# An encoder layer on one core: the recurrence's operands in the space of the projections' input, and a 512-column matmul for the memories

## The chip, the cores and the metric

The kernel runs on one core of one Trainium2 chip. The metric is the device time of one execution in microseconds (us); a lower time is better. Two sequences, one of 512 tokens and one of 256, go through the layer together as 768 tokens. A difference of about 1% (16 us) is what a measurement of this kernel can tell from no change.

## What is computed

One encoder layer: a mixer (an RWKV-7 recurrence on half of the channels, gated linear attention, "GLA", on the other half), a cross attention to a memory of 256 rows for each sequence, and a feed-forward network, each between two RMS norms. The reference, cut to what matters here:

```python
def hybrid_mixer(h, p):
    proj = h @ p['w_in']
    rw = centred_shift(proj[..., :R_COLS], p['mu_prev'], p['mu_next']).astype(jnp.float32)
    gl = proj[..., R_COLS:].astype(jnp.float32)
    mixed = jnp.concatenate([rwkv7_group(rw, p), gla_group(gl, p)], axis=-1).astype(h.dtype)
    return mixed @ p['w_out']

def rwkv7_scan(r, w, k, v, kk, a):
    def step(S, inp):
        r_t, w_t, k_t, v_t, kk_t, a_t = inp
        sa = jnp.einsum('bhij,bhj->bhi', S, -kk_t)
        S = (S * w_t[:, :, None, :] + sa[..., None] * (kk_t * a_t)[:, :, None, :]
             + v_t[..., None] * k_t[:, :, None, :])
        return S, jnp.einsum('bhij,bhj->bhi', S, r_t)
    ...

def cross_attention(h, m, p):
    q = (h @ p['wq_x']).reshape(B, S, X_HEADS, X_HD)
    kv = (m @ p['wkv_x']).reshape(B, M, 2, X_HEADS, X_HD)
    ...

def encoder_trunk(x, mem, params):
        x = x + rms_norm(hybrid_mixer(rms_norm(x, p['g_mix_pre']), p), p['g_mix_post'])
        m = rms_norm(mem, p['g_mem'])
        x = x + rms_norm(cross_attention(rms_norm(x, p['g_x_pre']), m, p), p['g_x_post'])
        h = rms_norm(x, p['g_ffn_pre'])
        x = x + rms_norm(jnp.square(jax.nn.relu(h @ p['w_ff1'])) @ p['w_ff2'], p['g_ffn_post'])
```

The model width is 1024, the feed-forward width 4096. The recurrence has 8 heads of 64 channels and runs forward and backward in time; GLA has 4 heads.

## The kernel before

Every large product is done in split precision: an operand becomes a high part (`split`, line 143: a copy on ACT to fp32r) and a low part (a subtraction, on POOL or DVE, line 148), and `mm3` (line 241) issues three matmuls, high by high, high by low, low by high, for each 128 rows of the contraction.

The work of the mixer comes in these pieces:

- **Projections.** The normed input lies channels first in the tiles `hT_hi` and `hT_lo` (8 blocks of 128 channels by 768 tokens each, in the pool `hp`). A projection block (`rkv_early`, `gla_dense`) multiplies them by 128 columns of `w_in`: 24 matmuls of 512 columns and 24 of 256. There are 24 such blocks; `blocks` calls them in the order of its list.
- **A pair of recurrence heads, p = 0 to 3.** `begin(p)` makes decays and scaled keys (`prep`, `bonus`) and the matrices `low` (line 685); `invert(p)` inverts 32-by-32 triangles by 31 pairs of DVE operations that each wait for the one before (lines 744 and 746); `joined(p)` puts the inverses together (matmuls of lines 788 and 800, DVE copies of line 803). Their results go to DRAM.
- **Products.** `products(p, g)`, called by `prods`, loads what group g of pair p needs into a "place", a set of five operands of 2560 elements a partition (chunk states, keys, inverses), and makes the chunk matrices `sca`, `scb`, `bktp`. There are six groups and so six places.
- **Stages, q = 0 to 4.** `stage(q)` runs four `step`s. A step of up to three jobs (pair q - 1 in its second third, pair q in its first and last third) goes PE, ACT (`rh`, line 1019), PE, ACT, PE, DVE (`t1`, line 1040), and the next step needs that result. There are 48 evacuations `rh` in all: 8 in stage 0, 12 in each of stages 1 to 3, 4 in stage 4.
- **GLA heads, h = 0 to 3.** `gla_head(h)` works in the tile `arena` of the pool `gp`, half of which each head overwrites two heads later: loads, exponentials on ACT, scans on DVE, matmuls `gs`, `gkt`, `gds`, `go`, `gsum`, and a gate; the result goes to DRAM (`mixd`).
- **Memories.** `memory()` loads the normed memories of both sequences, 512 columns, into `mem_hi` and `mem_lo` (pool `mq2`); `memory_block(mem, b)`, for 16 blocks b of 128 columns of `wkv_x`, multiplies them. Each block has 24 weights, and every weight is used by two matmuls of 256 columns that follow each other (line 1104, held in order by `order_after`).
- **Output projection.** `load_split` brings `mixd` (8 pairs of tiles) and `w_out` (32 quarters of 128 by 256) in; `out_projection` multiplies with 288 matmuls of 512 columns and writes the next `hT_hi` and `hT_lo`. Then follow queries, attention and the feed-forward network, which the diff does not touch.

Memory on chip sets much of the order. A pool that is opened where another one was closed waits for the last use of the tiles that lay there. Before the change the pools stand so: `gp` (the GLA heads) is closed, then `mq1` with the places 0, 4, 1, 5, 2 is opened in its space; after stage 0 has been written, `hp` (the projections' input) is closed and `mq2` with place 3, two accumulators `ya` and the memories is opened. In program text all four GLA heads stand ahead of the first products.

The text is only the start of the order. The framework's scheduler puts each engine's instructions into one fixed sequence by priorities (`tc.high_priority`, with offsets: 6000 for joins, 4000 for steps, 3000 for products, 2000 for `begin` and `invert`) and by its own estimate of time; on the chip each engine then runs its sequence strictly in order and waits where an operand is not there. All DMAs are issued by one engine, SP, also in order.

Of the kernel before, what the change touches and what calls it, by code (L numbers as in the profile page):

```python
# [16 lines left out]
P = 128  # L17
# [15 lines left out]
def kernel(ctx: ExitStack, tc: tile.TileContext, I, y_prompt, y_sample):  # L33
# [412 lines left out]
    def rkv_early(p, i):  # L446

        ot = hp.tile([P, T], F32, tag="gd", bufs=2, name="gd")
        rkv_block(p, i, lambda c, n: ot[:, c:c + n])
        dma(rkvd[p, i], ot)  # L450
        if i == 2:
            vt = tokens_first(ot)
            for h, hs in enumerate(HS):
                for par, ps_ in enumerate(HS):
                    dma(vtd[p][h][:, :, par * 64:par * 64 + 64], vt[ps_, :, hs])

    def tokens_first(ot):

        vt = hp.tile([P, T], F32, tag="gd", bufs=2, name="gd")
        for c, n in SEQS:  # L460
            pt = psd("gvt")
            for j in range(0, n, P):
                pe.transpose(out=pt[:, j:j + P], in_=ot[:, c + j:c + j + P], identity=ident)
            with tc.high_priority():
                dve.tensor_copy(out=vt[:, c:c + n], in_=pt[:, 0:n])
        return vt.rearrange("p (j e) -> p j e", e=P)

    def gla_dense(g, i):

        c0 = (1952, 2208, 2992, 2464)[g] + i * P  # L470
        w = load_block([(w_cols(c0, P), 0)], P)
        ot = hp.tile([P, T], F32, tag="gd", bufs=2, name="gd")
# [132 lines left out]
    mp = mp_cm.__enter__()  # L605
    tts, tdz = [], []
    for d in range(2):
        t = mp.tile([P, NCH, 64], F32, tag=f"tt{d}", name=f"tt{d}")
        pool.memset(t, 0.0)
        tts.append(t)  # L610
        tdz.append(mp.tile([P, NCH, 32], F32, name=f"tdz{d}"))
    px = mp.tile([P, NCH, 66], F32, tag="px", name="px")
# [339 lines left out]
    def open_places(pool_, gs):  # L952
        for g in gs:
            t = pool_.tile([P, 2560], F32, tag=f"pl{g}", name=f"pl{g}")
            places[g] = (t[:, 0:512].rearrange("p (h u x) -> p h u x", h=2, x=64),
                         t[:, 512:1280].rearrange("p (u i x) -> p u i x", u=4, x=64),
                         t[:, 1280:1792].rearrange("p (u h x) -> p u h x", u=4, x=64),
                         t[:, 1792:2304].rearrange("p (u x) -> p u x", x=P),
                         t[:, 2304:2560].rearrange("p (u x) -> p u x", x=64))

    mq1_cm = tc.tile_pool(name="mq1", bufs=1, reuse_waits="tile")
# [45 lines left out]
    def step(st, x, j, pc):  # L1007
# [54 lines left out]
        else:  # L1062
            dve.tensor_tensor(out=o, in0=y1, in1=o, op=ALU.add)
            dve.tensor_tensor(out=o, in0=y2, in1=o, op=ALU.add)

    def finish(st, seqs=SEQS, tiles=None, mixed=None):

        p, pa = st["p"], st["ya"]
        pb, bon, gt = tiles or (mq2.tile([P, T], F32, tag="fb", name="fb"),) * 3
        a, b = seqs[0][0], seqs[-1][0] + seqs[-1][1]  # L1070
# [26 lines left out]
    def memory_block(mem, b):  # L1097

        w = load_block([(wkv[:, b * P:(b + 1) * P], 0)], P)
        pd, prev = psd("pd"), None  # L1100
        for k, (wh, wl) in enumerate(w):
            for i, (x, y) in enumerate(((wh, mem[k][0]), (wh, mem[k][1]), (wl, mem[k][0]))):
                for c0 in (0, 256):
                    prev = order_after(pe.matmul(  # L1104
                        out=pd[:, c0:c0 + 256], lhsT=x, rhs=y[:, c0:c0 + 256],
                        start=(k + i + c0 == 0), stop=(k + i + c0 == KD + 257)), prev)
        if b >= KD:
# [56 lines left out]
    joined(2)  # L1164
    invert(3)
    for b in range(16):
        memory_block(mem, b)
    stage(1)
    with tc.high_priority(offset=2000):
# [16 lines left out]
    mo = [mp.tile([P, T], F32, tag="lsb", bufs=4, name="mo") for _ in range(2)]  # L1186
    tiles = (mq2.tile([P, T], F32, tag="fb", name="fb"), *mo)
# [5 lines left out]
    mq2_cm.__exit__(None, None, None)  # L1193
    hp_cm = tc.tile_pool(name="hp2", bufs=1, side="right", reuse_waits="tile")
    hp = hp_cm.__enter__()
    for k in order:
        if k != 3:
            load_split(mixd[k], *mix[k], lo_eng=pool)
    planes = []
# [3 lines left out]
    for g in (0, 4, 1, 5):  # L1203
        t = mq1.tile([P, 5, 512], F32R, tag=f"pl{g}", name=f"w_pl{g}")
        planes += [t[:, i, :] for i in range(5)]
    planes += [mq1.tile([P, 512], F32R, tag="bkg", bufs=3, name="w_bkg") for _ in range(3)]
    t = mq1.tile([P, 5, 512], F32R, tag="pl2", name="w_pl2")
    planes += [t[:, i, :] for i in range(5)]
    wt = {}
    for i, k in enumerate(order):  # L1210
# [78 lines left out]
    with tc.tile_pool(name="op1", bufs=1, reuse_waits="tile") as op1:  # L1289
        g_pre = gain_row(op1, "g_x_pre")  # L1290

        xn = [[op1.tile([P, 512], F32, name="xn")], [t[:, 512:T] for t in mo]]
        mo = [t[:, 0:512] for t in mo]

        def rows():
            return ((rk.tile([P, T], F32, tag="k", name="res0")[:, 0:512], mq1.tile([P, T], F32, tag="ya0", name="res1")[:, 0:512]), mo, xn)

        hT_hi, hT_lo = out_projection(op1, wt, mix, x_rows, rows, g_post, x1d, g_pre)
    mq1_cm.__exit__(None, None, None)
    mp_cm.__exit__(None, None, None)  # L1300
    rk_cm.__exit__(None, None, None)
# [441 lines left out]
```

## Time and profile before

| | |
|---|---|
| median of 3 runs | 1591.46 us (1590.47 to 1599.93) |
| the profiled execution | 1596.87 us, of which its span is 1595.0 us |
| mean granted TensorE clock | 0.914 |
| ACT, POOL busy | 718.9 us (45%), 514.6 us (32%) |
| DMA | 250.35 MB, mean 157 GB/s |

PE is TensorE's matmul, PEld its weight load, which overlaps; DVE, ACT and POOL are the vector, scalar and GpSimd engines. A matmul counts as busy until its result has drained, so PE's busy share is above its share of useful work: matmuls start before their predecessors end. "PEclk" is the share of the full TensorE clock that was granted. In a row of a window, x is the number of instructions; in a row of a tile or line, the three durations are least, median and largest in ns, then come the first and the last start in us from the span's start, then shapes.

### The profile page before, as it was taken

Reading aid. Unit: us, or ns where it says so; the run is one execution under the profiler, and the core shown is the slowest. Engines: PE = TensorE matmul, PEld = TensorE weight load, DVE = VectorE, ACT = ScalarE, POOL = GpSimd, SP = SyncE. Lnnn points to the kernel's source line nnn. Section 1 sums busy time; section 2 is a strip of 40 time slices with the busy share of each in tenths; the row PEclk is TensorE's granted clock in tenths of the full one; section 3 lists DMA queues with packets and bytes.
Section 4 is the critical chain, followed back from the end, with each engine's and each line's share of the span. In section 5 each row is a group of like instructions: output and inputs, shape, how many; then the busy total and the mean of one; then the engine's idle time right before and its main releaser. Section 6 shows DMA issues by size and latency. Waiting matters only on the chain. (4 is left out here: it accounts for less than half of the span.)

```text
span 1595.0 us, 28271 instructions
## 1 busy us (share of the span) xinstructions
PE 1442.8 (90%) x10614; PEld 1246.0 (78%) x10614; DVE 1049.7 (66%) x1605; ACT 718.9 (45%) x1417; POOL 514.6 (32%) x576
## 2 busy tenths in 40 slices
PE   7999689889887889899888999996999999999996
PEld 6887578777775777778767888786999999787785
DVE  5545885497577795764455434448876676878886
ACT  5754344443333332333344354434555556544442
POOL 6416643494317342211531354420000001231223
PEclk9999798989875988888979999997999999999998
DMA  6686555556468447754452333235555447564434
GB/s 168 181 302 188 167 137 131 145 146 192 111 205 229 127 149 176 205 134 135 126 166 99 119 95 105 73 111 160 172 169 176 158 145 284 171 204 132 143 100 142
DMA packets 279565, 250.35 MB, mean 157 GB/s; under 512 B 89264, under 2 KB 227059, under 8 KB 279428
## 3 DMA queue, kind: packets, MB, share of 16 engines
q1 hardware_dynamic: 279428, 248.54, 52.1%
q8 instruction: 84, 1.38, 0.4%
q14 instruction: 53, 0.43, 0.1%
HBM read 164.11 MB, written 82.58 MB: 155 GB/s over the span
## 5 line engine op out<-in xcount | busy, mean ns | idle before, releaser
L148 POOL TENSOR_TENSOR wlo<-wraw,whi 128x256 fp32r<-128x256 f32 x192 | 176.8, 934 | 331.0 <-ACT whi L147 231.1
L247 PE MATMUL pd<-hT_hi,whi 128*128 128x256 f32 (+1 forms) x512 | 182.0, 356 | 12.6 <-DVE gd L325 8.2
L247 PE MATMUL pd<-hT_hi,wlo 128*128 128x512 f32 (+1 forms) x512 | 180.1, 354 | 4.0 <-POOL wlo L148 4.0
L247 PE MATMUL pd<-hT_lo,whi 128*128 128x256 f32 (+1 forms) x512 | 178.6, 350 | 0.3 <-DVE hT_lo L206 0.3
L1511 POOL TENSOR_TENSOR wl<-w,wh 128x1024 fp32r<-128x1024 f32 x8 | 21.2, 2649 | 329.8 <-ACT wh L1510 329.8
L247 PEld LDWEIGHTS pd<-hT_hi,whi 128*128 128x128 f32 x512 | 100.4, 196 | 27.6 <-issue 5.5
L247 PEld LDWEIGHTS pd<-hT_hi,wlo 128*128 128x128 f32 x512 | 99.6, 195 | 18.6 <-POOL wlo L148 5.3
L147 ACT ACTIVATE whi<-wraw 128x256 fp32r<-128x256 f32 x192 | 77.3, 414 | 78.2 <-PE pd L1104 22.9
L247 PEld LDWEIGHTS pd<-hT_lo,whi 128*128 128x128 f32 x512 | 100.4, 196 | 13.0 <-DVE hT_lo L206 0.5
L148 DVE TENSOR_TENSOR ul<-ur,uh 128x768 fp32r<-128x768 f32 x56 | 77.4, 1388 | 30.7 <-ACT uh L147 17.7
L147 ACT ACTIVATE uh<-ur 128x768 fp32r<-128x768 f32 x56 | 47.4, 847 | 107.8 <-PE gz L1520 52.0
L1510 ACT ACTIVATE wh<-w 128x1024 fp32r<-128x1024 f32 x64 | 67.1, 1053 | 35.9 <-PE fz L1520 24.2
L1520 PE MATMUL gx<-wh,uh 128*128 128x512 f32 x192 | 75.0, 397 | 4.3 <-DVE acc L1713 4.3
L1511 DVE TENSOR_TENSOR wl<-w,wh 128x1024 fp32r<-128x1024 f32 x56 | 68.2, 1219 | 15.1 <-ACT wh L1510 14.5
L1520 PE MATMUL gx<-wl,uh 128*128 128x512 f32 x192 | 75.9, 395 | 0.0
L1520 PE MATMUL gx<-wh,ul 128*128 128x512 f32 x192 | 75.4, 395 | 0.0
L1520 PE MATMUL fz<-hh,wh 128*128 128x384 f32 x192 | 66.0, 344 | 1.9 <-ACT wh L1510 1.9
L1511 POOL TENSOR_TENSOR wl<-ws,wh 128x1024 fp32r<-128x1024 f32 x16 | 40.6, 2536 | 79.6 <-ACT wh L1510 79.6
L1520 PE MATMUL fz<-hh,wl 128*128 128x384 f32 x192 | 65.2, 344 | 0.8 <-DVE wl L1511 0.8
L1520 PE MATMUL fz<-hl,wh 128*128 128x384 f32 x192 | 65.8, 343 | 0.0
L1510 ACT ACTIVATE wh<-ws 128x1024 fp32r<-128x1024 f32 x48 | 50.5, 1052 | 26.8 <-PE fx L1520 22.3
L1104 PE MATMUL pd<-mem_hi,whi 128*128 128x256 f32 x256 | 59.3, 308 | 1.4 <-ACT mo L1116 1.4
(476 smaller groups left out, 4306.9 us busy)
## 6 DMA issues: line engine op xcount, KB each, us to landing
w<-in_w_ff_dram SPq DMA_DIRECT2D x64, 512.0 KB
ur<-ud SPq DMA_DIRECT2D x56, 384.0 KB
wraw<-in_w_in_dram SPq DMA_DIRECT2D x108, 128.0 KB
ud<-u SPq DMA_DIRECT2D x32, 384.0 KB
ud<-us SPq DMA_DIRECT2D x24, 384.0 KB
wraw<-in_wkv_x_dram SPq DMA_DIRECT2D x64, 128.0 KB
lora<-lo_t SPq DMA_DIRECT2D x20, 384.0 KB
bkg<-bkd SPq DMA_DIRECT2D x24, 256.0 KB
```

The costliest lines, as they stand in the source:

```text
L147: act.activation(out=hi, in_=src, func=AF.Copy)
L148: (lo_eng or pool).tensor_tensor(out=lo, in0=src, in1=hi, op=ALU.subtract)
L247: pe.matmul(out=out, lhsT=a, rhs=b, start=(i == 0), stop=(i == n - 1))
L1104: prev = order_after(pe.matmul(out=pd[:, c0:c0 + 256], lhsT=x, rhs=y[:, c0:c0 + 256], start=(k + i + c0 == 0), stop=(k + i + c0 == KD + 25 ...
L1510: act.activation(out=hi, in_=t[name], func=AF.Copy)
L1511: lo_eng.tensor_tensor(out=lo, in0=t[name], in1=hi, op=ALU.subtract)
L1520: pe.matmul(out=out, lhsT=a, rhs=b, start=first and i == 0, stop=last and i == n - 1, skip_group_check=True)
```

## The change

It moves tiles, and with them work:

- The places 0, 4, 1, 5 and most of place 3 are cut out of two tiles that take over the tags, and so the space, of `hT_hi` and `hT_lo`; place 2 and a piece of place 3 stay in `mq1`, now on the right side of the memory. So `hp` is not closed, and the products wait for the last projection block instead of for the last GLA head.
- In the text the last three projection blocks stand inside the list of the blocks; `gla_head(2)`, `begin(2)`, `invert(2)` and `gla_head(3)` move from among the blocks to behind `stage(0)`, with the products of place 3. Only then is `gp` closed and `mq2`, with the memories alone, opened in its space.
- `memory_block` calls `mm3` on all 512 columns: 24 matmuls a block in place of 48.
- After the sixteenth memory block `mq2` is closed, and 18 of the 32 halves of `w_out` get tiles of their own in its space (`wo1`); before, 20 lay in the places 0, 4, 1, 5. Accumulators `ya`, `xn` and a residual row move to the projection blocks' `gd` tiles, `fb` to `sxf`.

The diff, cut:

```diff
+    gdp_cm = tc.tile_pool(name="gdp", bufs=1, side="right", reuse_waits="tile")
+    gdp = gdp_cm.__enter__()
...
-    with tc.tile_pool(name="gp", bufs=1, reuse_waits="tile") as gp:
+    gp_cm = tc.tile_pool(name="gp", bufs=1, reuse_waits="tile")
+    gp = gp_cm.__enter__()
+    if True:
...
         blocks([(5, i) for i in range(3)])
-        gla_head(2)
         blocks([(3, 3), (2, 3)])
-        begin(2)
-        invert(2)
-        gla_head(3)
+        blocks([(6, i) for i in range(3)])
...
-    open_places(mq1, (0, 4, 1, 5, 2))
-    yas = [mq1.tile([P, T], F32, tag="ya0", name="ya0")]
+    plh, pll = (hp.tile([P, KD * T], F32, tag=n, name="pl_" + n) for n in ("hh", "hl"))
+    for t, gs in ((plh, (0, 4)), (pll, (1, 5))):
+        for i, g in enumerate(gs):
+            whole_place(g, t[:, 2560 * i:2560 * i + 2560])
+    place(3, plh[:, 5120:5632], pll[:, 5120:5888], mq1.tile([P, 512], F32, tag="pl3", name="pl3"), plh[:, 5632:6144],
+          pll[:, 5888:6144])
+    whole_place(2, mq1.tile([P, 2560], F32, tag="pl2", name="pl2"))
+    yas = [gdp.tile([P, T], F32, tag="gd", bufs=2, name=f"ya{i}") for i in range(2)]
...
-        pd, prev = psd("pd"), None
-        for k, (wh, wl) in enumerate(w):
-            for i, (x, y) in enumerate(((wh, mem[k][0]), (wh, mem[k][1]), (wl, mem[k][0]))):
-                for c0 in (0, 256):
-                    prev = order_after(pe.matmul(
-                        out=pd[:, c0:c0 + 256], lhsT=x, rhs=y[:, c0:c0 + 256],
-                        start=(k + i + c0 == 0), stop=(k + i + c0 == KD + 257)), prev)
+        pd = psd("pd")
+        mm3(pd, list(zip(w, mem)))
...
     prods(0, (0, 4, 1, 5))
-    blocks([(6, i) for i in range(3)])
     stage(0)
-    prods(0, (2,))
-    hp_cm.__exit__(None, None, None)
+    prods(0, (2, 3))
+    gla_head(2)
+    begin(2)
+    invert(2)
+    gla_head(3)
+    gp_cm.__exit__(None, None, None)
     mq2_cm = tc.tile_pool(name="mq2", bufs=1, reuse_waits="tile")
     mq2 = mq2_cm.__enter__()
-    open_places(mq2, (3,))
-    yas += [mq2.tile([P, T], F32, name=f"ya{i}") for i in (1, 2)]
-    prods(0, (3,))
     mem = memory()
     begin(3)
     joined(2)
     invert(3)
     for b in range(16):
         memory_block(mem, b)
+    mq2_cm.__exit__(None, None, None)
     stage(1)
...
+    wo1_cm = tc.tile_pool(name="wo1", bufs=1, reuse_waits="tile")
+    wo1 = wo1_cm.__enter__()
+    planes = [wo1.tile([P, 512], F32R, name=f"w_out{i}") for i in range(18)]
```

What the scheduler makes of it shows best on PE. The lists below are PE's sequence; names are those of the tiles (`pd<-hT...` a projection, `gsum`, `gs`, `gds`, `go` of a GLA head, `low` of `begin`, `merge` of a join, `rec` a step), then the size of the result and a count. Ahead of the change, the last GLA head's sums stand among projections:

```order
L247 MATMUL pd<-hT_hi,wlo 128x256
L247 MATMUL pd<-hT_hi,whi 128x256
L921 MATMUL gsum<-arena,ones_f 128x512
L921 MATMUL gsum<-arena,ones_f 128x256
L247 MATMUL pd<-hT_lo,whi 128x256
L247 MATMUL pd<-hT_hi,wlo 128x256
L247 MATMUL pd<-hT_hi,whi 128x256
```

After it, behind stage 0, the sums of head 2 stand between small matmuls of `begin(2)`, `begin(3)` and head 3:

```order
L880 MATMUL gkt<-ident,arena 128x128 x6
L926 MATMUL gsum<-arena,ones_f 128x512
L926 MATMUL gsum<-arena,ones_f 128x256
L688 MATMUL low<-bk 64x64 x8
L867 MATMUL gs<-arena 64x64 x24
L634 MATMUL hsum<-kds,ones_bd 128x512
L903 MATMUL gds<-arena 128x128 x8
```

Two heads have left the projections; no projection and no memory matmul stands beside them any more. The second place is PE's first memory matmul. Before, it stands among `low` and products, ahead of stage 1:

```order
L1049 MATMUL rec<-pl_4468 64x64 x4
L991 MATMUL sca<-pl_4467,bkg 64x64
L992 MATMUL scb<-pl_4467,bkg 64x64
L685 MATMUL low<-bk 64x64
L1104 MATMUL pd<-mem_hi,whi 128x256 x2
L1104 MATMUL pd<-mem_lo,whi 128x256 x2
L685 MATMUL low<-bk 64x64 x14
```

Now it stands in the midst of stage 1, behind all of `low`, head 3 and the join of pair 2:

```order
L1032 MATMUL rec<-pl_hh 64x64 x4
L1040 MATMUL rec<-rh,pl_hh 64x64 x4
L1058 MATMUL rec<-pl_4232 64x64 x4
L249 MATMUL pd<-mem_hi,whi 128x512
L249 MATMUL pd<-mem_lo,whi 128x512
L1047 MATMUL rec<-pl_hh 64x64 x8
L1009 MATMUL bktp<-ident,bkg 128x64 x8
```

All memory blocks have moved behind it, and a row holds one matmul where it held two. The third place is the end of stage 4. Before, PE has output projection (`po<-`) between the last steps:

```order
L1023 MATMUL rec<-pl_5344 64x64 x4
L1031 MATMUL rec<-rh,pl_5344 64x64 x4
L247 MATMUL po<-w_pl_9176,mix_wc 128x512
L247 MATMUL po<-w_pl_9177,mix_wc 128x512
L247 MATMUL po<-w_pl_9176,mix_r 128x512
```

After, the steps follow the last memory matmul with nothing between, and `po` begins behind them:

```order
L249 MATMUL pd<-mem_hi,wlo 128x512
L1058 MATMUL rec<-pl_4232 64x64 x4
L1120 MATMUL kvt<-ident,mo 128x128 x4
L1027 MATMUL rec<-pl_hh,pl_hl 64x64 x4
L1032 MATMUL rec<-pl_hl,pl_hh 64x64 x4
L1040 MATMUL rec<-rh,pl_hl 64x64 x4
L1047 MATMUL rec<-pl_hh,pl_4231 64x64 x4
L1058 MATMUL rec<-pl_hh 64x64 x4
```

So the output projection has left stage 4. Counted in the same sequences: of the 48 step evacuations, 8 stand ahead of the first memory matmul before the change and 14 after it; of the 1152 matmuls of the projection blocks, 478 stand behind the join of pair 0 before, and 513 after; behind the first memory matmul up to the last step stand 384 memory matmuls and 1114 others after the change.

More of the change, by code (lines that the diff above doesn't have):

```diff
@@ L446, in rkv_early @@
     def rkv_early(p, i):
-        ot = hp.tile([P, T], F32, tag="gd", bufs=2, name="gd")
+        ot = gdp.tile([P, T], F32, tag="gd", bufs=2, name="gd")
         rkv_block(p, i, lambda c, n: ot[:, c:c + n])
@@ L457, in tokens_first @@
     def tokens_first(ot):
-        vt = hp.tile([P, T], F32, tag="gd", bufs=2, name="gd")
+        vt = gdp.tile([P, T], F32, tag="gd", bufs=2, name="gd")
         for c, n in SEQS:
@@ L471, in gla_dense @@
         w = load_block([(w_cols(c0, P), 0)], P)
[L472 removed]
+        ot = gdp.tile([P, T], F32, tag="gd", bufs=2, name="gd")
         for c, n, pd in channels_product(w, P, hT_hi, hT_lo):
@@ L605 @@
     mp = mp_cm.__enter__()
-    tts, tdz = [], []
+    tdz = mp.tile([P, 2, NCH, 32], F32, tag="tdz", name="tdz")
+    tdz = [tdz[:, d] for d in range(2)]
+    tts = []
     for d in range(2):
@@ L942, with place, whole_place @@
         blocks([(5, i) for i in range(3)])
-        gla_head(2)
         blocks([(3, 3), (2, 3)])
-        begin(2)
-        invert(2)
-        gla_head(3)
+        blocks([(6, i) for i in range(3)])
     places = {}
[L952 to L961, printed above, removed]
-    mq1 = mq1_cm.__enter__()
-    open_places(mq1, (0, 4, 1, 5, 2))
-    yas = [mq1.tile([P, T], F32, tag="ya0", name="ya0")]
+    mq1_cm = tc.tile_pool(name="mq1", bufs=1, side="right", reuse_waits="tile")
+    mq1 = mq1_cm.__enter__()
+    def place(g, xv, a_, bkt, rbk, tp):
+        places[g] = (xv.rearrange("p (h u x) -> p h u x", h=2, x=64), a_.rearrange("p (u i x) -> p u i x", u=4, x=64),
+                     bkt.rearrange("p (u h x) -> p u h x", u=4, x=64), rbk.rearrange("p (u x) -> p u x", x=P),
+                     tp.rearrange("p (u x) -> p u x", x=64))
+    def whole_place(g, t):
+        place(g, *(t[:, a:b] for a, b in ((0, 512), (512, 1280), (1280, 1792), (1792, 2304), (2304, 2560))))
+    plh, pll = (hp.tile([P, KD * T], F32, tag=n, name="pl_" + n) for n in ("hh", "hl"))
[6 more added lines that the diff above has]
+    yas = [gdp.tile([P, T], F32, tag="gd", bufs=2, name=f"ya{i}") for i in range(2)]
     def bc2(ap):
@@ L1064, in step, with finish_tile @@
             dve.tensor_tensor(out=o, in0=y2, in1=o, op=ALU.add)
+    def finish_tile():
+        return mp.tile([P, D], F32, tag="sxf", name="fb")[:, 0:T]
     def finish(st, seqs=SEQS, tiles=None, mixed=None):
         p, pa = st["p"], st["ya"]
-        pb, bon, gt = tiles or (mq2.tile([P, T], F32, tag="fb", name="fb"),) * 3
+        pb, bon, gt = tiles or (finish_tile(),) * 3
         a, b = seqs[0][0], seqs[-1][0] + seqs[-1][1]
@@ L1165 @@
     invert(3)
+    yas.append(mp.tile([P, T], F32, tag="kds", name="ya2"))
     for b in range(16):
         memory_block(mem, b)
+    mq2_cm.__exit__(None, None, None)
     stage(1)
@@ L1186 @@
     mo = [mp.tile([P, T], F32, tag="lsb", bufs=4, name="mo") for _ in range(2)]
-    tiles = (mq2.tile([P, T], F32, tag="fb", name="fb"), *mo)
+    tiles = (finish_tile(), *mo)
     with tc.high_priority(offset=2000):
@@ L1202 @@
         planes += [t[:, 0, :], t[:, 1, :]]
-    for g in (0, 4, 1, 5):
-        t = mq1.tile([P, 5, 512], F32R, tag=f"pl{g}", name=f"w_pl{g}")
-        planes += [t[:, i, :] for i in range(5)]
+    planes.append(mp.tile([P, T], F32R, tag="tdz", name="w_tdz")[:, 0:512])
     planes += [mq1.tile([P, 512], F32R, tag="bkg", bufs=3, name="w_bkg") for _ in range(3)]
@@ L1208 @@
     planes += [t[:, i, :] for i in range(5)]
+    planes.append(mq1.tile([P, 512], F32R, tag="pl3", name="w_pl3"))
     wt = {}
@@ L1290 @@
         g_pre = gain_row(op1, "g_x_pre")
-        xn = [[op1.tile([P, 512], F32, name="xn")], [t[:, 512:T] for t in mo]]
+        xn = [[gdp.tile([P, T], F32, tag="gd", bufs=2, name="xn")[:, 0:512]], [t[:, 512:T] for t in mo]]
         mo = [t[:, 0:512] for t in mo]
         def rows():
-            return ((rk.tile([P, T], F32, tag="k", name="res0")[:, 0:512], mq1.tile([P, T], F32, tag="ya0", name="res1")[:, 0:512]), mo, xn)
+            return ((rk.tile([P, T], F32, tag="k", name="res0")[:, 0:512], gdp.tile([P, T], F32, tag="gd", bufs=2, name="res1")[:, 0:512]), mo, xn)
         hT_hi, hT_lo = out_projection(op1, wt, mix, x_rows, rows, g_post, x1d, g_pre)
+    wo1_cm.__exit__(None, None, None)
     mq1_cm.__exit__(None, None, None)
+    gdp_cm.__exit__(None, None, None)
     mp_cm.__exit__(None, None, None)
```

5 lines of the change are left out of this document (removed).

## The prediction

> **What bounds the kernel now.** I read the page's head first, then a table of windows cut at the stages, then rows of single tiles.
>
> ```profile
> span 1595.0 us, 28271 instructions
> ...
> PE 1442.8 (90%) x10614; PEld 1246.0 (78%) x10614; DVE 1049.7 (66%) x1605; ACT 718.9 (45%) x1417; POOL 514.6 (32%) x576
> ```
>
> PE is busy 90%, but busy counts draining. What a matmul really occupies is the distance to the next start:
>
> ```profile
> 100.06 0.40 PE L247 MATMUL pd<-hT_hi,whi 128*128 128x512 f32 x1
> 100.30 0.39 PE L247 MATMUL pd<-hT_lo,whi 128*128 128x512 f32 x1
> 100.53 0.39 PE L247 MATMUL pd<-hT_hi,wlo 128*128 128x512 f32 x1
> 100.76 0.28 PE L247 MATMUL pd<-hT_hi,whi 128*128 128x256 f32 x1
> 100.88 0.28 PE L247 MATMUL pd<-hT_lo,whi 128*128 128x256 f32 x1
> 101.00 0.28 PE L247 MATMUL pd<-hT_hi,wlo 128*128 128x256 f32 x1
> ```
>
> 512 columns take 0.23 to 0.24 us, 256 columns 0.12. The window table (us; busy and count of PE, PEld, DVE, ACT, POOL; PEclk; DMA share; GB/s) and the marks show where PE runs like that and where it doesn't:
>
> ```profile
> 288.00:443.00 155.00, 138.00 (x1031) 116.61 (x1026) 111.19 (x146) 64.83 (x117) 81.29 (x70) 0.88 0.56 152
> 443.00:503.00 60.00, 45.27 (x641) 36.74 (x639) 45.79 (x85) 23.90 (x68) 24.04 (x22) 0.66 0.75 215
> 503.00:636.00 133.00, 118.35 (x1553) 101.20 (x1554) 100.58 (x211) 43.60 (x118) 54.69 (x48) 0.83 0.60 160
> 636.00:692.00 56.00, 48.76 (x629) 42.54 (x624) 44.59 (x128) 21.91 (x59) 12.08 (x16) 0.91 0.64 183
> 692.00:745.00 53.00, 49.06 (x674) 40.94 (x673) 22.61 (x58) 16.93 (x45) 5.83 (x8) 0.77 0.56 138
> 817.00:893.00 76.00, 71.58 (x336) 56.65 (x336) 38.64 (x69) 29.03 (x77) 12.18 (x24) 0.98 0.36 116
> 893.00:1595.00 702.00, 663.02 (x3369) 587.42 (x3367) 472.03 (x585) 338.49 (x572) 152.24 (x164) 0.97 0.45 149
> ...
> L247 PE MATMUL pd<-hT_hi,wlo x384: 274/390/795, 61.9 to 442.2; 128*128 128x512 f32 x96, 128*128 128x256 f32 x96
> L1031 PE MATMUL rec<-rh,pl x384: 218/218/362, 445.7 to 820.4; 64*64 64x64 f32 x192
> L1104 PE MATMUL pd<-mem_hi,whi x256: 274/281/581, 503.0 to 789.3; 128*128 128x256 f32 x128
> ...
> 440.87 1.11 DVE L803 COPY tt<-merge 32x384 f32<-32x384 f32 x2 [1.00 <-PE merge L800]
> 444.58 1.13 DVE L803 COPY tt<-merge 32x384 f32<-32x384 f32 x2
> ...
> 288.18 1.12 DVE L803 COPY tt<-merge 32x384 f32<-32x384 f32 x2 [0.68 <-PE merge L800]
> 631.64 1.11 DVE L803 COPY tt<-merge 32x384 f32<-32x384 f32 x2 [1.89 <-PE merge L800]
> 644.09 1.13 DVE L803 COPY tt<-merge 32x384 f32<-32x384 f32 x2
> ```
>
> Projections end at 442. The joins of pairs 0, 1 and 2 end at 289, 446 and 645 (the last two `tt` copies of each). Steps run from 446 to 820, memory matmuls from 503 to 789; the output projection fills most of 817 to 893. Behind 893 the diff touches nothing (702 us stay). From 443 to 636 DVE is busy 146.4 of 193 us: there the chain of `begin`, inverse and join on DVE sets the pace, and memory matmuls lie beside it.
>
> **The change part by part.** All marks below are of the span of 1595.0 us.
>
> *512 columns.* 768 matmuls at 0.12 become 384 at 0.235: 92 against 90 us. I take 2 us off PE; bounds 0 and 4. The rule that speaks otherwise is a rival, below.
>
> *Heads 2 and 3 leave the projections.* Their price on each engine comes from all instructions on `arena`, four heads:
>
> ```profile
> 130.00:432.00 302.00, 62.93 (x472) 54.85 (x472) 75.52 (x52) 73.64 (x100) 27.93 (x36) 0.86 0.55 145
> 286.17 1.33 DVE L932 TENSOR_TENSOR arena<-arena 128x768 f32<-128x768 f32 x1
> 367.10 0.95 DVE L932 TENSOR_TENSOR arena<-arena 128x768 f32<-128x768 f32 x1
> 430.37 1.31 DVE L932 TENSOR_TENSOR arena<-arena 128x768 f32<-128x768 f32 x1
> ```
>
> One head is 15.7 us of PE, 18.9 of DVE, 18.4 of ACT; two fall out of 288 to 443. PE: 513 projection matmuls remain behind the join of pair 0 (half of each width, 0.177 us on average): 91 us, and small matmuls, about 15, so 289 + 106 = 395 at the earliest. Latest is 442, no gain. DVE: 111.2 - 37.8 = 73.4 us, which at its share of that window (111.2 of 155) takes 102: 391, and the join behind the inverse still waits for DMAs. I take 408, nearer to the lower end, as both engines have a bound near 395: **-35** at the end of the projections and at the join of pair 1.
>
> *Places in the space of `hT`.* Loads of the first place can no longer be issued under the last projections; they wait for their last matmul, then for six DMAs that SP issues one behind the other. Before, stage 0 began 3 us behind the projections; I give it 9 (bounds 3 and 20): **+6**, so 418.
>
> *Two heads behind stage 0.* From join 1 to join 2 DVE had 146 us of work over 193 (443 to 636). Counted in its sequence, the same stretch now holds the two heads (+38) but only 7 `t1` in place of 17 and fewer products (about -35): the length stays, and join 2 comes at 601, with the late start at **606** against 636 (taking 636, the end of the first copies and of DVE's work, as mark). Bounds 580, where DVE waits for nothing, and 640.
>
> *The memories start late.* They wait for head 3's result to go out, then 16 splits:
>
> ```profile
> L148 POOL TENSOR_TENSOR mem_lo<-raw,mem_hi x16: 718/727/2177, 485.4 to 512.8; 128x256 fp32r<-128x256 f32 x16
> ```
>
> 16 at 0.73 are 12 us, with DMA and gate 20: memory begins at **626**, not 503. The cover that stage 0, `low` and the joins had from memory matmuls is gone; PE is nearly empty from stage 0's end (about 462) to 626, which costs nothing there, as DVE sets that stretch, but the 90 us must then go into the rest.
>
> *What PE has behind 626.* 384 x 0.235 = 90 us, and 1114 small matmuls. Their price is the rest of a window less its memory part:
>
> ```profile
> 636.00:692.00 56.00, 28.40 (x179) 25.10 (x180) 0.91 0.64 183
> 692.00:745.00 53.00, 17.26 (x104) 14.66 (x102) 0.77 0.56 138
> ```
>
> (48.76 - 28.40) / 450 = 45 ns and (49.06 - 17.26) / 570 = 56 ns: 50 to 62 us. So 140 to 152 us, 146; at the 90% of these two windows (97.8 of 109) 162: the last memory matmul at **788**, against 790. Two steps and a bit remain. Stage 3 and stage 4 give the length of a step:
>
> ```profile
> 745.18 0.28 ACT L1019 ACTIVATE rh<-rec 128x128 f32<-128x128 f32 x1 [1.10 <-PE rec L1018]
> 777.52 0.28 ACT L1019 ACTIVATE rh<-rec 128x128 f32<-128x128 f32 x1
> 781.06 0.28 ACT L1019 ACTIVATE rh<-rec 128x128 f32<-128x128 f32 x1 [2.21 <-PE rec L1018]
> 816.30 0.28 ACT L1019 ACTIVATE rh<-rec 128x128 f32<-128x128 f32 x1
> ```
>
> 32.3 us for four steps, 8 each: 788 + 17 = **805** for the last step against 820, **-15**. (Stage 4 took 12 a step, with output projection between; that is gone.)
>
> *The output projection.* Before, it had begun inside stage 4; now all 288 matmuls (288 x 0.235 = 68 us) follow it, and `w_out` has to wait for the memory tiles' space:
>
> ```profile
> L147 ACT ACTIVATE w_pl<-raw x24: 400/418/420, 806.2 to 825.8; 128x256 fp32r<-128x256 f32 x24
> ```
>
> These splits came as late before (806 to 826, for a last memory matmul at 790), so the wait is not new. 805 + 68 + 5 of transposes + 5 to the first split pair is 883; with stalls as before (71.6 busy of 76) 887, against 893: bounds 875 and 905. So the loss here is 9 of the 15 us gained.
>
> *Sum.* Projections -35, start of stage 0 +6, join 2 at -30; the recurrence keeps that, but the memories, 123 us late, take it back but for 15; output projection +9; the rest 0, 512 columns inside the 146: 887 - 893 = -6, and -2 for residual rows now loaded early, which I only allow 0 to 3: **-8**. The profiled execution took 1596.87 with its span of 1595.0; the median of the three runs is 1591.46, 5.4 lower. I put the difference on the median: 1591.5 - 8 = **1583**.
>
> **Rivals.**
>
> *A, faster: the recurrence alone sets the end.* If PE slips memory matmuls into the waits of steps without delaying them, 626 to 788 shrinks. Inverse 3 and stage 1 end some 59 us after join 2 (665; between 636 and 692 it took 56), then stages 2 and 3 at 32 and stage 4 at 40 us: 665 + 104 + 5 = 774, less than 805 by 31, so 1583 - 30 = 1553. For it: PE's sequence has such gaps at every step. Against it: PE had 90 to 93% busy in the windows at 636 and 692 already, with half as much memory work. The Trainium skill gives it another ground: "TensorE: Matmul & The Clock Gate", section "Back-to-back issue gap", puts sustained matmuls of 512 columns at about 131 ns; memory would then be 50 us, not 90, and the sum about 1544 to 1553. The trace has 0.23 to 0.24 for the same thing, so I give that ground nothing; A lives from the first.
>
> *B, slower: the stretch without cover gets long.* The two heads now run one behind the other with nothing dense on PE. The windows show the clock that PE then gets:
>
> ```profile
> 480.00:520.00 40.00, 28.63 (x287) 23.56 (x283) 28.03 (x41) 15.18 (x40) 31.39 (x29) 0.54 0.87 236
> ...
> L1019 ACT ACTIVATE rh<-rec x8: 277/278/278, 444.9 to 489.1; 128x128 f32<-128x128 f32 x8
> ```
>
> Heads 2 and 3 ended 81 and 63 us behind the one before. Stage 0 took 44 us and so ends at 418 + 44 = 462; two heads at 81 + 63 or at 81 each, and the 20 of splits and DMA, end at 626 to 644. At 0.54 in place of 0.86 a head's 15.7 us of PE become 25, 19 more for two: 645 to 663, 19 to 37 late, 28 in the middle: 1583 + 28 = 1611. It decides from a memory start at about 650. Against it: DVE has 96 us of other work in that stretch, behind which PE's slowness hides. The same page, section "What's actually happening", says that the clock halves after an idle window of some 3.4 us and comes back after a busy one of that length; 0.54 agrees with it, and by it the whole stretch would run at half, which is B's condition.
>
> *C, the projections do not get shorter:* bound by weight splits or by `begin(1)`, they end at 430 to 443, and all later marks move: 1583 + 25 = 1608. Against it: the two bounds near 395.
>
> **How the numbers follow.** My forecast, 1583 (1566 to 1600 by the bounds of its terms), has a chance of 0.42; A 0.27 (1540 to 1570); B 0.20 (1600 to 1622); C 0.11 (1598 to 1618). Faster by over 1% is below 1575.5, slower above 1607.4; 1% is about what a measurement of this kernel can tell from no change. Faster: A 0.27 and 0.10 of the forecast, 0.37. Slower: 0.14 of B, 0.06 of C, 0.20. The same: 0.43. The range 1551 to 1614 leaves out some 0.10 of A below and 0.08 of B and C above.
>
> **What would show it.** Last projection matmul near 408; the join of pair 2's first copies near 606; first memory matmul (128x512) near 626 at 0.235 us apart, last near 788; last `rh` near 805; first queries near 887. PE below half busy from 465 to 620. A shows as a last memory matmul before 765; B as a first one after 650; C as projections past 430. What would make it wrong is a wait in neither list: SP's DMAs for the places, queued behind ones that wait.

## The result, and the profile after

The changed kernel takes 1675.24 us (median of 4, 1667.85 to 1677.75) against 1593.98 us for the kernel before on the same chip (median of 4): a ratio of 1.0498, 95% interval 1.0448 to 1.0548. It is 5% slower, some 81 us. The forecast was 1583 us, 8 less than before, with a range of 1551 to 1614; the measured time lies outside it.

The head of the page after, with the row of PE's clock and its busy tenths in 40 slices of 41.9 us:

```profile
span 1675.4 us, 27534 instructions
...
PE 1454.5 (87%) x10230; PEld 1229.3 (73%) x10230; DVE 1047.8 (63%) x1605; ACT 719.0 (43%) x1417; POOL 499.1 (30%) x576
...
PE   7997689869957566899997999997899999999996
...
PEclk9998597989655555789997999999899999999998
```

Busy times are close to those of before; the span has grown. From 461 to 670 us (the twelfth to the sixteenth slice) PE is five to seven tenths busy at about half its clock. The marks:

| mark, us of the span | before | forecast | after |
|---|---|---|---|
| last projection matmul | 442 | 408 | 430 |
| first `rh`, stage 0 | 445 | 418 | 440 |
| last `rh` of stage 0 | 489 | 462 | 506 |
| first `rh` of stage 1 | 531 | not named | 629 |
| join of pair 2, first copies | 632 | 606 | 626 |
| first memory matmul | 503 | 626 | 661 |
| last memory matmul | 790 | 788 | 873 |
| last `rh` | 816 | 805 | 883 |
| first queries | 893 | 887 | 973 |

Windows of the changed kernel cut at its marks (columns as in the prediction):

```profile
439.00:506.00 67.00, 46.83 (x544) 38.35 (x544) 46.69 (x73) 17.18 (x46) 19.11 (x12) 0.50 0.51 143
506.00:661.00 155.00, 96.23 (x976) 77.59 (x972) 119.53 (x193) 53.89 (x107) 46.38 (x46) 0.56 0.44 116
661.00:730.00 69.00, 58.02 (x762) 44.41 (x758) 37.29 (x108) 20.43 (x63) 12.57 (x16) 0.72 0.44 111
730.00:873.00 143.00, 142.93 (x1631) 108.54 (x1630) 62.97 (x183) 62.92 (x173) 41.92 (x60) 0.99 0.48 142
873.00:973.00 100.00, 84.30 (x419) 65.30 (x420) 51.74 (x97) 39.42 (x104) 30.81 (x55) 0.88 0.43 136
973.00:1676.00 703.00, 662.45 (x3369) 585.94 (x3367) 472.56 (x586) 338.31 (x572) 152.31 (x164) 0.97 0.46 149
```

Behind 973 nothing has changed (703 us, before 702). Between the projections and the queries lie 543 us, before 451 (442 to 893). The windows show two stretches that no longer lie beside each other: from 439 to 661 DVE is busy for 166 of 222 us, and PE for 143 at about half its clock, with no memory matmul among its work; from 730 to 873 PE is busy for 142.93 of 143 us at a clock of 0.99. Following the waits back, each instruction to what released it or else to the one before it on its engine, gives the chain of each stretch by engine, in us:

```
back from the first memory matmul to 434 us: DVE 113, PE 51, DMA 29, ACT 15, issue 15, other 8
back from the last step to 661 us:           PE 183, DMA 19, DVE 15, other 7
```

What lies between shows in single rows. The first `rh` of stage 1, by ACT's timeline (start, duration, in brackets the idle time before it and what ended it):

```profile
628.71 0.28 ACT L1028 ACTIVATE rh<-rec 128x128 f32<-128x128 f32 x1 [0.45 <-PE rec L1027]
```

The matmuls `go` of the heads, whose last are those of head 3, by the rows of `arena`:

```profile
L918 PE MATMUL go<-arena x96: 314/474/529, 198.6 to 630.4; 128*128 128x64 f32 x96
```

PE's timeline has the matmuls of that first step between them:

```profile
627.42 0.61 PE L918 MATMUL go<-arena 128*128 128x64 f32 x2
627.97 0.70 PE L1027 MATMUL rec<-pl 128*64 128x64 f32 x8
628.60 0.80 PE L918 MATMUL go<-arena 128*128 128x64 f32 x2
```

And the memories, by the rows of `mem_hi`:

```profile
L249 PE MATMUL pd<-mem_hi,whi x128: 388/396/799, 661.2 to 872.1; 128*128 128x512 f32 x128
...
L150 POOL TENSOR_TENSOR mem_lo<-raw,mem_hi x16: 772/880/942, 647.5 to 660.0; 128x256 fp32r<-128x256 f32 x16
```

From 506 to 628 no step of the recurrence runs, though pair 1 had been joined at 425 and its products made by 542. The first step of stage 1 runs among the last `go` of head 3; and the memories, whose space waits for head 3, follow. Their splits begin at 647, when head 3's result has gone out (644.6). Their first matmul needed only the first of these splits and its weights, which were there at 654.8; it came at 661 because a step stands ahead of it in PE's order, and that step waited for DVE:

```profile
660.56 0.69 PE L1058 MATMUL rec<-pl 128*64 128x64 f32 x8 [3.57 <-DVE t L1049]
661.19 0.80 PE L249 MATMUL pd<-mem_hi,whi 128*128 128x512 f32 x1
```

### The profile page after: what moved, and what is told of

It is laid out like the page before. It is cut to its first block, busy times and chain, and to the rows that moved or that the text cites. A ratio compares the mean times of both kernels' runs of the same rounds, so it can differ in the third digit from the quotient of the medians.

```text
span 1675.4 us, 27534 instructions
## 1 busy us (share of the span) xinstructions
PE 1454.5 (87%) x10230; PEld 1229.3 (73%) x10230; DVE 1047.8 (63%) x1605; ACT 719.0 (43%) x1417; POOL 499.1 (30%) x576
## 5 line engine op out<-in xcount | busy, mean ns | idle before, releaser
L150 POOL TENSOR_TENSOR wlo<-wraw,whi 128x256 fp32r<-128x256 f32 x192 | 160.7, 849 | 329.7 <-ACT whi L149 259.7
L249 PE MATMUL pd<-hT_hi,wlo 128*128 128x256 f32 (+1 forms) x512 | 179.1, 352 | 2.3 <-POOL wlo L150 2.3
L747 DVE TENSOR_TENSOR stmp<-sqf,snf 112x31 f32<-112x31 f32 (+15 forms) x124 | 55.0, 444 | 3.1
```

Of the source, the lines that this page charges most:

```text
L150: (lo_eng or pool).tensor_tensor(out=lo, in0=src, in1=hi, op=ALU.subtract)
L249: pe.matmul(out=out, lhsT=a, rhs=b, start=(i == 0), stop=(i == n - 1))
L747: dve.tensor_tensor(out=tm, in0=sq[:, 0:nr, j:j + 1].broadcast_to([112, nr, ni]), in1=sn[:, j:j + 1, j + 1:32].broadcast_to([112, nr, ni]) ...
```

## The experiments

Theory O (order), from the result: the loss comes from heads 2 and 3 behind stage 0 and from the memories behind them, since the recurrence and the memories then come late and PE has too much left behind 661. Theory P: the matmuls of 512 columns, or the places in the space of `hT`, cost the time. Later runs split O. Ratios are to the kernel before on the same chip.

**Heads early.**

```diff
         blocks([(5, i) for i in range(3)])
+        gla_head(2)
         blocks([(3, 3), (2, 3)])
+        begin(2)
+        invert(2)
+        gla_head(3)
         blocks([(6, i) for i in range(3)])
...
-    gla_head(2)
-    begin(2)
-    invert(2)
-    gla_head(3)
     gp_cm.__exit__(None, None, None)
```

> The changed kernel, with GLA heads 2 and 3 and begin and invert of pair 2 back among the projection blocks as before the change, and the pool of the GLA heads closed there; places in the space of the projections' input, 512 columns and everything else stay changed. Theory O (order): the 81 us come from the two heads and the memories standing behind stage 0, so that 434 to 661 us holds little but DVE's chain and 661 to 884 holds all of PE's memory work. Then memory begins at 470 to 500 in place of 661, the last rh is near 820 in place of 884, and the time is 1575 to 1610. Rival P (places and 512 columns): the loss is in the matmuls of 512 columns that stand between steps, or in the places that must wait for the projections; then it stays at 1650 or above.

Measured: 1596.23 us, ratio 1.0021 (1.0001 to 1.0040). The rows of `mem_hi`, and windows of the same stretch as in the changed kernel:

```profile
L249 PE MATMUL pd<-mem_hi,whi x128: 389/396/796, 489.0 to 754.9; 128*128 128x512 f32 x128
```

```profile
462.00:560.00 98.00, 80.01 (x803) 61.23 (x804) 69.29 (x129) 36.14 (x94) 51.69 (x48) 0.79 0.72 202
560.00:660.00 100.00, 84.95 (x1093) 65.04 (x1093) 84.31 (x163) 33.19 (x92) 41.30 (x35) 0.83 0.64 172
660.00:756.00 96.00, 82.32 (x1115) 62.11 (x1106) 53.31 (x155) 33.01 (x94) 20.90 (x32) 0.93 0.55 145
```

Memory begins at 489, PE is over 80% busy beside DVE's work, the last `rh` is at 813, queries start at 893. All but some 3 us of the loss is gone with this one edit, while places and 512 columns stay; P falls as the cause of the 81 us.

**Two matmuls of 256 columns again**, in the changed kernel, and **512 columns alone**, in the kernel before:

```diff
-        pd = psd("pd")
-        mm3(pd, list(zip(w, mem)))
+        pd, prev = psd("pd"), None
+        for k, (wh, wl) in enumerate(w):
+            for i, (x, y) in enumerate(((wh, mem[k][0]), (wh, mem[k][1]), (wl, mem[k][0]))):
+                for c0 in (0, 256):
+                    prev = order_after(pe.matmul(
...
```

> The changed kernel with the memories multiplied in two matmuls of 256 columns again, as before the change. Theory O: 384 matmuls of 0.235 us are 90 us, 768 of 0.12 are 92, and PE sets the pace there, so 0 to 5 us slower: 1672 to 1682. Rival P: long matmuls in front of the steps cost more than they save; then it is 15 us or more faster, 1660 or below.

> The kernel before with the 512-column matmul of the memories alone, nothing moved. Theory O: -4 to +2 us against the kernel before (2 us less PE work, beside DVE's chain for most of its length), 1587 to 1596. Rival P: over 10 us slower, since each matmul in front of a step is twice as long.

Measured: 1692.76 us in the changed kernel (ratio 1.0625, 1.0597 to 1.0652), 17 us slower than with 512 columns; and 1586.45 us for the kernel before with 512 columns alone, ratio 0.9966 (0.9944 to 0.9989). The 17 us are far above my 2 us and outside O's 0 to 5; the gain in the old order, 6 us by the medians, is 2 to 9 by its interval. P, by which long matmuls cost time, falls in both. The rows of the memory matmuls alone, of the run with 256 columns (first) and of the changed kernel:

```profile
661.00:890.00 229.00, 115.72 (x768) 98.91 (x768) 0.92 0.46 129
```

```profile
661.00:873.00 212.00, 109.16 (x384) 72.29 (x384) 0.91 0.47 132
```

6.6 us of the 17 are PE's busy time on the memory matmuls themselves (their weight loads double as well, 768 against 384); the last memory matmul comes 17 us later and the output projection 18 (917 against 898.5). The other 10 go with what stands between the memory matmuls in the new sequence: all steps now stand ahead of the last one (the last `rh` is at 849), and the stretch holds 2856 - 768 = 2088 other records against 2390 - 384 = 2006. Why the scheduler orders it so was not taken apart.

The 512 columns alone, in the old order, are the one version that is faster than the kernel before, by 0.3%, which only many runs can tell. Against it, the run with heads early, which adds the places in the space of `hT`, is 10 us slower (the two intervals do not overlap): the places are not free. The recurrence begins at 478 there, at 445 with 512 columns alone.

**Memory matmuls thinned.**

```diff
-        mm3(pd, list(zip(w, mem)))
+        for k, (wh, wl) in enumerate(w):
+            pe.matmul(out=pd, lhsT=wh, rhs=mem[k][0], start=(k == 0), stop=(k == KD - 1))
```

> The changed kernel with two of the three matmuls of each memory weight left out (only high by high remains: 128 of 384 matmuls of 512 columns); this part of the computation is missing, loads and splits stay. It takes 256 x 0.235 = 60 us off PE behind 661 us and nothing else. Theory O says that PE sets the pace from the first memory matmul to the last step: 45 to 60 us faster, 1615 to 1632. Rival S (the recurrence's own steps set it, with PE waiting in turn): at most 20 us faster, 1655 or above.

Measured: 1638.49 us, 37 less, between both forecasts: the stretch from the first to the last memory matmul is 173 us in place of 212, 39 of the 60 us. PE sets most of that stretch; the other third does not arrive. PE now idles more and runs at a lower clock, which goes with that, though what each of the two costs was not measured. The window from the first to the last memory matmul of this run has a clock of 0.79, against 0.91 in the changed kernel, and 19 us without PE, against 11:

```profile
660.00:833.00 173.00, 154.38 (x2041) 116.65 (x2040) 98.21 (x273) 76.87 (x224) 52.81 (x73) 0.79 0.56 156
```

**Heads early, memories late.** Heads 2 and 3 as in the first run, but the pool of the heads is closed behind a small copy out of pair 2's joined tiles, so the memories get its space only then (the diff is against that run):

```diff
-    gp_cm.__exit__(None, None, None)
-    mq2_cm = tc.tile_pool(name="mq2", bufs=1, reuse_waits="tile")
-    mq2 = mq2_cm.__enter__()
-    mem = memory()
     begin(3)
     joined(2)
+    pool.tensor_copy(out=arena[0:32, 0:32], in_=tts[0][0:32, 0, 32:64])
+    pool.tensor_copy(out=arena[0:32, 32:64], in_=tts[1][0:32, 0, 32:64])
+    pool.tensor_copy(out=arena[0:32, 9 * T:9 * T + 32], in_=arena[0:32, 0:32])
+    gp_cm.__exit__(None, None, None)
+    mq2_cm = tc.tile_pool(name="mq2", bufs=1, reuse_waits="tile")
+    mq2 = mq2_cm.__enter__()
+    mem = memory()
     invert(3)
```

> The run with heads 2 and 3 early, but the space of the GLA heads is given to the memories only behind the join of pair 2 (three small POOL copies out of the joined tiles into the heads' tile hold it). So heads are early and memories late. Theory M: what costs is that the 90 us of memory matmuls find PE only from about 660 us on, and PE sets the pace from there. Then the first memory matmul is at 650 to 690, the last step and the end come late again, 1630 to 1670 in place of 1596. Rival H: what costs are the two heads on DVE's chain behind stage 0, and the memories would fit in late as well; then 1590 to 1612.

**Begin late.** Only `begin(2)` and `invert(2)` stay behind stage 0; `gla_head(2)` and `gla_head(3)` stand behind the last projection block in the text:

```diff
         blocks([(6, i) for i in range(3)])
+        gla_head(2)
+        gla_head(3)
...
-    gla_head(2)
     begin(2)
     invert(2)
-    gla_head(3)
     gp_cm.__exit__(None, None, None)
```

> The changed kernel with GLA heads 2 and 3 moved ahead of stage 0 (the order then has them among the projections), while begin and invert of pair 2 stay behind stage 0; the memories can begin at once. Theory M: memory begins at 480 to 510, time 1588 to 1615. Rival D (the late chain of begin, invert and join of pair 2 on DVE is what costs, whatever PE has beside it): 1640 or above.

Measured: 1634.56 us (ratio 1.0255, 1.0235 to 1.0276) with memories late, 1608.31 us (1.0080, 1.0049 to 1.0110) with `begin(2)` late. In both the memories begin where M has them (657 and 507) and the time is in M's range; H and D fall. A late `begin(2)` still costs some 10 us against the run with heads early. With heads early and memories at 657, nearly the 661 of the changed kernel, the time is 41 us below the changed kernel's and 38 above that of heads and memories early: late memories make 38 us, the rest comes from the heads' place in another way. The stretch from the first to the last memory matmul of the run with memories late, first all work and then the memory matmuls alone (PE, PEld, PEclk, DMA share, GB/s):

```profile
657.00:832.00 175.00, 168.14 (x1835) 128.05 (x1835) 94.36 (x241) 73.55 (x198) 57.95 (x77) 0.95 0.50 141
```

```profile
657.00:832.00 175.00, 100.49 (x384) 71.08 (x384) 0.95 0.50 141
```

1835 - 384 = 1451 records of other matmuls are left there; in the changed kernel, whose window of the same stretch is in the next fence, 2390 - 384 = 2006. The difference, 555, at (168.14 - 100.49) / 1451 = 47 ns is 26 us of the 37 by which the stretch is shorter. Here 24 of the 48 `rh` lie ahead of the first memory matmul, in the changed kernel 14. All work of the changed kernel from its first to its last memory matmul:

```profile
661.00:873.00 212.00, 200.95 (x2390) 152.95 (x2388) 100.27 (x291) 83.35 (x235) 54.49 (x76) 0.91 0.47 132
```

**The clock.** 160 matmuls with unused results between the steps of stage 0:

```diff
+    def fill(n, prev):
+        pd = psd("fill")
+        for i in range(n):
+            prev = order_after(pe.matmul(out=pd[:, 0:P], lhsT=ident, rhs=ident, start=True, stop=True), prev)
...
                     step(st, x, j, pc)
+                    if q == 0:
+                        fill(20, gate[0])
```

> The changed kernel with 160 idle matmuls (identity by identity, 128 columns, result unused) between the steps of stage 0, 20 behind each job of a step. Rival K (clock): stage 0 took 66 us, against 44 before, since PE ran at half its clock there; with the clock up it is 10 us or more shorter, memory begins at 651 or earlier, and the time is 1665 or less. Theory M: the granted clock rises in 440 to 506, but DVE and DMAs set that stretch, and the idle matmuls stand in front of others: memory begins between 658 and 685, time 1672 to 1700.

Measured: 1697.97 us (1.0652, 1.0625 to 1.0679). The window of stage 0 in this run:

```profile
439.00:506.00 67.00, 61.07 (x731) 54.27 (x732) 39.95 (x76) 15.08 (x42) 11.25 (x8) 0.90 0.49 141
```

The clock is 0.90 in place of 0.50, and stage 0 runs from 446 to 511 us, 65 us against 66; memory begins at 672. K falls: stage 0 was not 10 us shorter. But the filling matmuls also stand in front of others, so a smaller gain that they took back is not excluded. Behind stage 0 the clock of this run is low again (0.61 from 506 to 585, 0.52 from 585 to 661), so what half the clock costs between stage 0 and the memories was not tried.

**`w_out` early**, on top of heads early: 20 of its 32 quarters and `mixd` of the GLA heads are loaded ahead of stage 4 in the text.

> The run with heads 2 and 3 early, and 20 of the 32 quarters of w_out loaded and split ahead of stage 4, since the memories are done at 756 us there and the splits came only at 818. If the end behind 756 waits for w_out: output projection begins by 800 among the last steps, 8 to 18 us faster than that run, 1578 to 1588. If the last steps set it: the matmuls put between them give back what they save, 1590 to 1600.

Measured: 1602.19 us (1.0042, 1.0016 to 1.0069), above both forecasts; by the ratios it is some 3 us above the run with heads early, with overlapping intervals. The output projection began at 766, but the last `rh` moved from 813 to 829: the steps behind the new matmuls gave back at least what was saved.

**The accumulators.** The scheduler gives tiles of one tag out in the order of the text. The tiles that matmuls write to lie in a memory of their own, PSUM. `gkt` and `go` of a head come from the three PSUM tiles that `rec` of the steps uses, and `gs`, `gds`, `gsum` from the two that the products use. Two runs take them from the projections' two, idle there:

```diff
-                pt = psy("gkt")
+                pt = (psd if h > 1 else psy)("gkt")
...
-                po = psy("go")
+                po = (psd if h > 1 else psy)("go")
```

> The changed kernel, heads 2 and 3 behind stage 0 as in it, but their tiles gkt and go come from the two PSUM tiles of the projections (idle there) in place of the three that they share with the steps' rec. Theory R (rotation): stage 1's rec tiles stand in the text behind those of head 3 in the same rotation of three, so no step of stage 1 can run before go of head 3 is read (its first rh was at 629, right among those matmuls). Then the first rh of stage 1 comes at 545 to 580, some 24 of the 48 rh lie ahead of the first memory matmul (14 before), which itself comes at 655 to 690; with so much less left for PE behind it, 1630 to 1655. Rival D (DVE's work holds stage 1 as well): first rh of stage 1 behind 610, time 1665 or above.

The second, on top of it:

```diff
-            pfb = [psm("gs").rearrange("p (c t) -> p c t", t=64)[:, 0:6] for _ in range(2)]
+            pfb = [(psd if h > 1 else psm)("gs").rearrange("p (c t) -> p c t", t=64)[:, 0:6] for _ in range(2)]
...
-                    pt = psm("gds").rearrange("p (c e) -> p c e", e=P)
+                    pt = (psd if h > 1 else psm)("gds").rearrange("p (c e) -> p c e", e=P)
...
-                pt = psm("gsum")
+                pt = (psd if h > 1 else psm)("gsum")
```

> As the run before, and gs, gds and gsum of heads 2 and 3 from the projections' PSUM tiles too, in place of the two that they share with the products sca and scb. Theory R: head 2's gs also waits in rotation, behind the products that stage 0 puts ahead of it (first gs at 542); freed, heads 2 and 3 run beside stage 0 and the first memory matmul is at 590 to 640: 1605 to 1640. Rival D: DVE and the half clock hold the heads; first memory at 655 or later, and the time within 8 us of the run before.

Measured: 1670.22 us (1.0482, 1.0443 to 1.0520) and 1646.93 us (1.0333, 1.0302 to 1.0365). The first `rh` of stage 1, by ACT's timeline of the first run and of the second:

```profile
533.01 0.61 ACT L1028 ACTIVATE rh<-rec 128x128 f32<-128x128 f32 x3 [0.23 <-PE rec L1027]
```

```profile
558.66 0.61 ACT L1028 ACTIVATE rh<-rec 128x128 f32<-128x128 f32 x3 [2.99 <-PE rec L1027]
```

533 and 559 against 629: the shared accumulators did hold stage 1, as R says. But R's times were too low: the first run lies on the side of D by its time, 1665 or above, and the second between R and D in time and start (647). In the first run 22 `rh` lie ahead of the memories, yet the steps now stand in front of head 3, its sums come at 662 (634 before), and memory begins at 690. Windows of this run up to there, and from there to the last memory matmul:

```profile
506.00:690.00 184.00, 124.50 (x1427) 101.53 (x1424) 144.50 (x294) 61.45 (x134) 44.10 (x45) 0.56 0.44 113
690.00:867.00 177.00, 175.64 (x1944) 132.26 (x1943) 70.71 (x196) 77.83 (x213) 51.92 (x72) 0.99 0.48 141
```

DVE is busy for 144.50 us before it, 25 more than in the changed kernel (119.53, from 506 to 661), and the second stretch shortens to 177 us but starts 28 later; 5 us are left, which the intervals of this run and of the changed kernel do not tell from nothing. In the second run heads 2 and 3 have their sums at 521 and 583, memory begins at 647, and the time is 28 us below the changed kernel: a third of the way back, with the heads where the change put them. There the memories' splits end at 625, 42 us behind head 3's sums, and their matmuls stand behind others in PE's order until 647; what sets this was not tried.

## Why the prediction was wrong

**The step that failed is "1114 small matmuls" behind the first memory matmul.** The 1114 were counted in PE's sequence of the program, and priced at 45 to 56 ns from windows of the profile. But the profile has two records for each plain fp32 matmul of the program. The 48 evacuations `rh` are each used by 4 matmuls of the program, 192 in all; the trace has 192 + 128 + 64 = 384:

```profile
L1040 PE MATMUL rec<-rh,pl_hl x192: 218/218/366, 478.7 to 884.5; 64*64 64x64 f32 x192
L1040 PE MATMUL rec<-rh,pl_hh x128: 218/218/366, 441.1 to 806.9; 64*64 64x64 f32 x128
L1040 PE MATMUL rec<-rh,pl x64: 218/218/311, 633.2 to 864.2; 64*64 64x64 f32 x64
```

All 896 matmuls of the steps are 1792 records. From the first memory matmul to the last step the trace holds 2084 records other than the memory's: 144 of transposes, one for each, and 1940 others, two for each, and 144 + 970 are the 1114. A price per record was put on a count of something else. The row of the changed kernel gives (200.95 - 109.16) / 2006 = 46 ns for the records up to the last memory matmul: the price was right and the count 1.8 times too small (1.9 up to the last step). With it the stretch is 90 + 92 to 112 = 182 to 202 us, at 90% busy 202 to 225, against 162 forecast and 212 measured. This term alone puts the last memory matmul from 788 to about 840 and the forecast, with all else as it was, to some 1635.

**The memories' start** came at 661, not 626. Two terms made this, 22 us each, and the stretch behind them gave 9 back. The projections ended at 430, not 408: a shorter list had been taken as dense, but PE stood idle where heads had filled in. Its two longest waits there, by PE's timeline:

```profile
315.37 0.69 PE L465 MATMUL gvt<-ident,gd 128*128 128x128 f32 x2 [7.05 <-ACT gd L477]
347.27 1.98 PE L688 MATMUL low<-bk 64*64 64x64 f32 x32 [9.55 <-DVE bk L675]
```

Both bounds near 395 left out these waits; rival C's end (430 to 443) is what happened. Stage 0 took 66 us, not the 44 taken over from before; with the clock up in the fill run it took as long, and what makes it longer stays open. The length of the stretch from stage 0's end to memory, 155 us against 164 forecast, was about right. DVE was the busiest engine there (119.53 of 155), as forecast, and has half of the chain back from the first memory matmul; what the half clock adds was not tried. The prediction let head 3 end with the join of pair 2: that join came at 626, head 3's last result at 644.5.

**What was in no list: the recurrence itself stood still.** I let the joins alone set when stages start, and took stage 1 to run beside the heads. Its first step came at 629, 98 us later than before, with pair 1 long joined. The two runs on accumulators show what held it: heads placed ahead of stage 1 in the text share with it the PSUM tiles of `rec`. So 34 of 48 `rh` were still to come when memory began, 40 before, although memory began 158 us later. This is no further term of the sum: the 1114 were counted in a sequence with 14 `rh` ahead of the memories, and the work of the other 34 is in them, at half its size. "The recurrence keeps that" held only for the join of pair 2 (626 against 632).

**The cover.** "PE is nearly empty ... which costs nothing there" was the wrong reading of a right row. PE's idle time there was no cost in that stretch, but the work that could have filled it was owed later: PE is 70% and then 62% busy at half its clock for 222 us, and from 730 on 142.93 of 143. The heads-early run puts 384 memory matmuls into 489 to 756 beside DVE's chain and is back at the level of before, though its recurrence starts 34 us later than before (478 against 445).

**The end.** From the last memory matmul to the first queries it took 100 us, against 99 forecast. The output projection took 75 us of it (898.5 to 973), about as forecast; the steps behind the memories were shorter than the 17 us forecast (11 to the last `rh`), and the wait for `w_out`, whose splits now start at 886.5, was longer: 26 us from the last memory matmul to the first `po` against 18 before. Behind 973: nothing, as forecast. The 512 columns: 2 us forecast; 17 in the changed kernel and 6 in the old.

**The rivals.** A fell: the last memory matmul came at 873, far behind its 765. Its second ground had no part in it: the Trainium skill, "TensorE: Matmul & The Clock Gate", section "Back-to-back issue gap", has about 131 ns for 512 columns. The trace does not agree for these fp32r operands: memory matmuls that follow each other stand 235 ns apart in the changed kernel at a clock of 0.99 (median of 274 distances between starts, 730 to 873 us). B named the right side and its own condition (memory behind 650) was met, but it put the price on the start alone, 28 us. Its cause, the half clock, did not show in the fill run for stage 0, and was not tried behind it. The Trainium skill, "TensorE: Matmul & The Clock Gate", section "What's actually happening", has the clock halved by an idle window and restored by a busy one. The rows agree in part: the clock is 0.50 with 544 records of PE in stage 0 and 0.90 with 731 in the filled one. But no run here shows that a single idle stretch does it: in the kernel before the clock was 1.00 from 443 to 462 us and 0.51 from 462 to 503, and PE's longest idle gap between 443 and 500 was 2.2 us.

C's end of the projections (430 to 443) came true, but its price, 25 us, was less than a third of the loss. Of the 86 us by which the first queries came later than forecast, the memories' start makes 35, the stretch behind it 50, and the end 1.

In sum, in this order of the runs: 1675 to 1635 us is what the late heads, with `begin(2)` and `invert(2)`, cost with memories nearly as late (661 and 657), 1635 to 1596 what late memories cost, and the places and 512 columns together leave the time where it was within 0.4%. Of the first step, freeing the accumulators of both kinds gives 28 us back, with memory 14 us earlier; how the rest splits between DVE's work in series, the clock and PE's order stays open.

## What to carry to other kernels

Before a count from a program's sequence is multiplied by a duration from a trace, one group of each kind has to be counted in both: here that would have shown x4 in one and x8 in the other. When work is moved in the text, list every rotating buffer, PSUM above all, that it shares with the work it is moved past: a rotation in text order made two independent chains one here (first step of stage 1 at 629 in place of 533), and no stage's own dependences show it. An engine that idles at no cost in one stretch pays for it later if its work was only postponed; what matters is how much of its work is left when the last producer lets go.

## What the runs showed of the hardware

A plain fp32 matmul of the program appears as two records in the trace (the 896 of the steps as 1792, the 160 filling ones of 128 columns as 320), and a transpose or a matmul of fp32r operands as one. Matmuls of 256 columns, two behind each other with one weight, load that weight twice (768 records of weight loads for 768 matmuls); two of them take 2 x 118 ns from start to start, the same as one of 512 (235 ns), but the whole stretch was 17 us longer. And with the granted clock raised from 0.50 to 0.90 by idle matmuls a stage took 65 us against 66, the cost of the filling included.
